# Attention maxima of two heads in the row halves of TensorE, transposed reciprocals, and one more leading column tile in a diffusion block

## The chip, the core and the metric

The kernel runs on one core of a Trainium2 chip. The metric is device time in microseconds for one execution. TensorE (PE in the profile) multiplies; loading its stationary operand is a separate instruction (PEld). VectorE (DVE), ScalarE (ACT) and GpSimd (POOL) do the elementwise work, and SyncE (SP) issues nearly all DMAs. Each engine runs its own instructions in program order and waits on semaphores for the others. TensorE writes into PSUM, eight banks of 128 partitions by 512 float32 words.

## What is computed

One layer of a block with two groups of heads, 1024 latent tokens, 256 context tokens, width 1024, head size 64. Group A is softmax attention with 8 query heads and 2 key heads; group B is a retention with 8 heads in chunks of 128. Both outputs go through one output projection, and a SwiGLU feed-forward network (FFN) of hidden width 2816 follows. All is float32. Cut to what matters here:

```
def gqa_block(q, k, v):
    qg = q.reshape(B, Q, ATTN_KV_HEADS, GQA_GROUP, HEAD_DIM)
    s = jnp.einsum('bqkgd,btkd->bkgqt', qg, k) * ATTN_SCALE
    p = jax.nn.softmax(s, axis=-1)
    o = jnp.einsum('bkgqt,btkd->bqkgd', p, v)
...
def swiglu(h, w_ffn_in, w_ffn_out):
    a, b = jnp.split(h @ w_ffn_in, 2, axis=-1)
    return (jax.nn.silu(a) * b) @ w_ffn_out
```

## The kernel before

Operands of the large products are split into a high part (rounded to float32r, which TensorE multiplies in one pass) and the remainder, the low part. Three products high·high, high·low and low·high add up to one float32 product (`mm3`, line 131). Plain float32 operands are also used in places, and then one matmul of the program is two records in the trace.

The stages that matter here, with their place in the profiled execution:

- **The last projections** (297.5 to 358.5 us). The input projection runs in column groups; the last of them are woven, step by step, with `front(0)` and `front(1)`. `front(h)` prepares one attention head. It splits the queries (`q3`, layout low, high, one more column), transposes them to `t1` (64 rows of low parts above 64 rows of high parts, line 581), and then finds for each of 1024 queries a maximum over all 1280 keys: 24 matmuls of `t1` against `K1`, whose 128 rows hold the high part of the keys twice (line 589), each followed by a reduction on VectorE (line 590). The negated maxima go into the last column of `q3` (lines 592 and 593), and a second set of transposes makes `t2` (line 598), whose 65th row carries the maximum into the scores.
- **Attention and retention** (358.5 to 704 us). Four pairs of heads `r`, two halves of queries, ten key tiles: `score` makes two accumulating matmuls per head (lines 625 and 626), ScalarE takes the exponential, `weigh` multiplies with the values, both heads of a pair in the two column halves of TensorE (line 634), `sums` adds up the denominators, and `normalise` turns the reciprocals over with a matmul against the identity (line 662) and multiplies. `front` for the next pair and the retention of four pairs of heads (`retain`, lines 741 to 812) are woven between. The retention multiplies two heads in the two row halves of TensorE (line 796, 64 rows each) and uses column halves too (lines 741, 808, 810).
- **Output projection** (704 to 804.5 us), for eight token tiles `mix_in`, `mix_out`, `residual`, `modulate`.
- **FFN** (from 804.5 us). The first matrix is multiplied with a scheme of seven products on half-size blocks per column tile `j`. Two of the seven (`first_product`, `second_product`) need only the tokens as they are; the other five need sums of token blocks (`Tx`), which VectorE splits first. Column tiles 0, 1 and 2 have their first two products done ahead of the rest, "leading"; the weights of tile 2 are in tiles named `lead`.

The instruction order is not written out. Code is written in the order of generators that `weave` advances by shares (`N_FR` is the number of steps of a `front`), and a scheduler then orders each engine's instructions by its own timeline; `tc.issue_after(x)` only makes the following instructions come later than x. All short-lived PSUM tiles (`sbank`) share four banks.

Of the kernel before, what the change touches and what calls it, by code (L numbers as in the profile page):

```python
# [11 lines left out]
F32 = mybir.dt.float32  # L12
F32R = mybir.dt.float32r
AF = mybir.ActivationFunctionType
ALU = mybir.AluOpType
# [4 lines left out]
P = 128  # L20
# [87 lines left out]
def hybrid_block(ctx: ExitStack, tc, x, c, cx, c_ctx, w_mod, b_mod, g_pre_mix, g_post_mix,  # L108
# [5 lines left out]
    def f(ap):  # L114
        return ap.bitcast(F32)
# [440 lines left out]
    def falloc(first, shape, dt, tag, bufs):  # L556
        if first == 1:
            return kvp.tile(shape, dt, name=f"{tag}b")
        if first == 0:
            return gp.tile(shape, dt, tag="g", name=tag)  # L560
        return atf.tile(shape, dt, tag=tag, name=tag, bufs=bufs)

    def front(h):

        kv = h // 4
        if h % 2 == 0:
            qs2[h // 2] = falloc(h, [P, LT, P], F32, "qs", 1)
            nc.sync.dma_start(out=qs2[h // 2], in_=d_p[0:N_LAT, h * HD:(h + 2) * HD].rearrange("(t p) n -> p t n", p=P))
        q3 = falloc(h, [P, LT, 2 * HD + 2], F32R, "q3", 2)
        qs = qs2[h // 2][:, :, (h % 2) * HD:(h % 2 + 1) * HD]  # L570
        S.copy(out=q3[:, :, HD:2 * HD], in_=qs)
        hold["q"] = V.tensor_tensor(out=q3[:, :, 0:HD], in0=qs, in1=f(q3[:, :, HD:2 * HD]), op=ALU.subtract)
# [4 lines left out]
        fr[h] = (t1, t2)  # L577
        for b in range(2):
            tb = sbank(F32R)
            for i in range(4):  # L580
                T.transpose(out=tb[:, i * P:(i + 1) * P], in_=q3[:, b * 4 + i, 0:P], identity=identr)
            S.copy(out=t1[:, b * 512:(b + 1) * 512], in_=f(tb))
            yield
        mx = small.tile([P, LT, 4], F32, tag="mx", name="mx")
        nm = small.tile([P, LT], F32, tag="nm", name="nm")
# [6 lines left out]
        V.tensor_reduce(out=nm, in_=mx[:, :, 0:3], axis=AX.X, op=ALU.max, negate=True)  # L592
        V.tensor_copy(out=q3[:, :, 2 * HD:2 * HD + 1], in_=nm.unsqueeze(2))
        yield
        for b in range(2):
            tb = sbank(F32R)
            for i in range(4):
                T.transpose(out=tb[:HD + 1, i * P:(i + 1) * P], in_=q3[:, b * 4 + i, HD:2 * HD + 1], identity=identr)
            S.copy(out=t2[:, b * 512:(b + 1) * 512], in_=f(tb[:HD + 1]))
            yield  # L600
# [253 lines left out]
    N_FR, N_RT, N_AT = 13, 47, 40  # L854
    attend = attention()
    retained = chain(*(retain(r) for r in range(4)))
    for n, fronts in ((N_AT, [2, 3]), (N_AT, [4, 5]), (N_AT, [6, 7])):
        n_r = n * 4 * N_RT // (3 * N_AT) + 1
        weave((islice(attend, n), n), (chain(*(front(h) for h in fronts)), len(fronts) * N_FR + 1),
              (islice(retained, n_r), n_r))  # L860
# [48 lines left out]
    up = ffs.enter_context(tc.tile_pool(name="up", bufs=3))  # L909
# [6 lines left out]
    def mix_in(t):  # L916

        tsl = slice(t * P, (t + 1) * P)
        rn = wk3.tile([P, 512], F32, tag="rn", name="rn", bufs=1)
        nc.sync.dma_start(out=rn, in_=d_r[tsl, :])  # L920
        mt = wk3.tile([P, 4, P], F32, tag="mt", name="mt", bufs=1)
        nc.sync.dma_start(out=mt, in_=d_m.rearrange("(k p) n -> p k n", p=P)[:, :, tsl])
        tb = sbank()
        for i in range(4):
            T.transpose(out=tb[:, i * P:(i + 1) * P], in_=rn[:, i * P:(i + 1) * P], identity=ident)
        rT = rTs[t] = wk3.tile([P, 2, KT, P], F32R, tag="rT", name="rT")
        split(rT[:, 0, 0:4], rT[:, 1, 0:4], mt, V)
        split(rT[:, 0, 4:8], rT[:, 1, 4:8], tb.rearrange("p (k n) -> p k n", n=P), S)
# [146 lines left out]
    raws[2] = [quarter(i, 2) for i in range(2)]  # L1075
# [7 lines left out]
    As[2] = [(hl[:, i, 0], hl[:, i, 1]) for i in range(2)]  # L1083
    N_EARLY = 3
# [15 lines left out]
    first_product(2)  # L1100
    second_product(2)
# [184 lines left out]
```

## Time and profile before

| what | value |
|---|---|
| time, median of 3 runs | 1494.71 us (1490.71 to 1501.16) |
| time of the profiled execution | 1494.64 us |
| its span, first to last instruction | 1492.9 us |
| TensorE busy | 1425.1 us (95%) |
| VectorE busy | 849.8 us (57%) |
| ScalarE busy | 525.8 us (35%) |
| GpSimd busy | 496.5 us (33%) |
| chain that ended last, TensorE's share | 80% |

Between span and time lie 1.7 us. A record's length is the latency of one instruction; matmuls overlap, so the pace of TensorE is read from the distance between starts.

### The profile page before, as it was taken

To read this page: it belongs to the slowest core of one execution; us is meant where nothing else is said; L and a number is where in the kernel's file an instruction comes from. 1 tells how busy PE (TensorE), PEld (TensorE's weight loads), DVE (VectorE), ACT (ScalarE), POOL (GpSimd) and SP (SyncE) were. 2 spreads that over 40 slices of the span, in tenths; PEclk is the share of its full clock that TensorE was granted. 3 is DMA by queue.
4 is the path that set the end of the run, shared out by engine and by line. 5 is a ranking of instruction groups with operands and counts; after the bars stand their busy time and mean duration, and the time that the engine had idled before them with its cause. 6 is when DMAs were issued, how large, how long until landed. Compare 5 with 4: busy or idle time off the path is not lost.

```text
span 1492.9 us, 19980 instructions
## 1 busy us (share of the span) xinstructions
PE 1425.1 (95%) x7354; PEld 1074.7 (72%) x7354; DVE 849.8 (57%) x1447; ACT 525.8 (35%) x1143; POOL 496.5 (33%) x402
## 2 busy tenths in 40 slices
PE   6999999898999999998998899999999999999997
PEld 2787877787555555544887688888888888888886
DVE  2666767545766677665556655444444454445445
ACT  3750221223655545455346423222222231113112
POOL 0112246401553636352016454444444430002003
PEclk9999999999999989999999999999999999999999
DMA  9456634314102111014334132222222225444562
GB/s 352 148 173 208 198 119 136 124 50 127 46 26 82 40 47 40 23 49 141 114 113 141 57 99 85 85 85 83 75 83 85 76 88 187 152 148 143 189 204 113
DMA packets 140624, 169.12 MB, mean 113 GB/s; under 512 B 8992, under 2 KB 90608, under 8 KB 140528
## 3 DMA queue, kind: packets, MB, share of 16 engines
q1 hardware_dynamic: 139680, 167.61, 34.6%
q8 instruction: 58, 0.95, 0.3%
q10 hardware_dynamic: 848, 0.25, 0.1%
q14 instruction: 38, 0.31, 0.1%
HBM read 132.17 MB, written 35.65 MB: 112 GB/s over the span
## 4 chain that ended last, share of the span: by engine, by line
PE 80%; DVE 8%; DMA 6%; ACT 2%; issue 2%; POOL 1%; SPq 0%; DVEq 0%; POOLq 0%; ACTq 0%
PE pb L131 48%; PE sb L131 15%; PE o L634 4%; PE sb L625 3%; PE sb L589 2%; DMA wm<-in_w_mod 2%; PE sb L626 2%; DMA raw<-in_w_out 1%; DVE ss L779 1%; PE r L796 1%; DVE mx L590 1%; PE r L741 1%; PE sb L808 1%; DMA rv<-d_p 1%; DMA raw<-in_w_in 1%
## 5 line engine op out<-in xcount | busy, mean ns | idle before, releaser
L131 PE MATMUL pb<-T,w 128*128 128x512 f32 x1320 | 315.2, 393 | 4.8 <-DVE T L126 2.1
L131 PEld LDWEIGHTS pb<-T,w 128*128 128x128 f32 x1320 | 246.9, 187 | 63.0 <-ACT w L125 2.6
L131 PE MATMUL pb<-whi,hT 128*128 128x512 f32 (+1 forms) x896 | 263.0, 374 | 5.3 <-ACT whi L125 3.6
L131 PEld LDWEIGHTS pb<-whi,hT 128*128 128x128 f32 x896 | 162.3, 190 | 40.3 <-ACT whi L125 4.5
L131 PE MATMUL pb<-wlo,hT 128*128 128x512 f32 (+1 forms) x448 | 165.4, 372 | 2.6 <-DVE wlo L126 2.6
L590 DVE TENSOR_REDUCE mx<-sb 128x1 f32<-128x512 f32 (+1 forms) x192 | 107.0, 594 | 53.4 <-PE sb L589 52.6
L126 DVE TENSOR_TENSOR w<-w1raw,w 128x512 fp32r<-128x512 f32 x152 | 123.3, 867 | 15.7 <-ACT w L125 15.7
L131 PE MATMUL sb<-B,w 128*128 128x512 f32 x504 | 124.9, 391 | 0.8 <-ACT u L1063 0.8
L125 ACT CAST w<-w1raw 128x512 fp32r<-128x512 f32 x152 | 83.7, 618 | 96.0 <-POOL w1raw L1010 94.4
L627 ACT ACTIVATE p<-sb 128x512 f32<-128x512 f32 x160 | 92.9, 599 | 68.2 <-PE sb L626 67.2
L131 PEld LDWEIGHTS sb<-B,w 128*128 128x128 f32 x504 | 94.4, 188 | 22.2 <-ACT u L1063 1.2
L682 POOL TENSOR_TENSOR acc<-acc,p 128x1024 f32<-128x1024 f32 x30 | 71.5, 2383 | 107.4 <-ACT p L627 103.1
L1142 POOL TENSOR_TENSOR g<-g,c 128x512 f32<-128x512 f32 x22 | 34.7, 1579 | 212.0 <-DVE c L1141 187.0
L131 PE MATMUL pb<-w,ah 128*128 128x512 f32 x328 | 101.7, 389 | 0.0
L131 PE MATMUL sb<-w,ah 128*128 128x512 f32 x328 | 101.5, 389 | 0.0
L131 PEld LDWEIGHTS pb<-wlo,hT 128*128 128x128 f32 x448 | 85.4, 191 | 19.4 <-DVE wlo L126 3.5
L634 PE MATMUL o<-p,VV 128*64 128x512 f32 x320 | 89.3, 637 | 5.1 <-ACT p L627 5.0
L176 POOL TENSOR_TENSOR ss<-ss,mhalf 128x1 f32<-128x1 f32 x26 | 15.0, 582 | 235.4 <-DVE ss L175 235.4
L125 ACT CAST w<-raw 128x512 fp32r<-128x512 f32 x41 | 25.4, 623 | 168.6 <-PE pb L131 152.8
L131 PE MATMUL pb<-woh,rT 128*128 128x512 f32 x256 | 82.3, 401 | 0.0
L125 DVE CAST ah<-ra 128x1024 fp32r<-128x1024 f32 x41 | 28.5, 698 | 88.7 <-PE pb L131 88.5
L319 POOL TENSOR_TENSOR st<-r,r 128x256 f32<-128x256 f32 (+1 forms) x32 | 42.3, 1323 | 90.0 <-DVE r L318 64.2
(258 smaller groups left out, 2470.3 us busy)
## 6 DMA issues: line engine op xcount, KB each, us to landing
w1raw<-in_w_ffn_in SPq DMA_DIRECT2D x92, 256.0 KB, 3.4
ra<-d_a SPq DMA_DIRECT2D x41, 512.0 KB, 4.3
wm<-in_w_mod SPq DMA_DIRECT2D x64, 256.0 KB, 3.2
raw<-in_w_ffn_out SPq DMA_DIRECT2D x41, 256.0 KB, 3.7
d_p<-st SPq DMA_DIRECT2D x34, 256.0 KB, 2.0
wm<-in_w_mod SPq DMA_DIRECT2D x16, 512.0 KB, 7.1
raw<-in_w_in SPq DMA_DIRECT2D x32, 256.0 KB, 4.3
d_a<-g SPq DMA_DIRECT2D x22, 256.0 KB, 2.0
```

What stands on the lines that cost most here:

```text
L125: a = S.copy(out=hi, in_=src) if hi_eng is S else hi_eng.tensor_copy(out=hi, in_=src)
L126: return a, V.tensor_tensor(out=lo, in0=src, in1=f(hi), op=ALU.subtract)
L131: T.matmul(acc, lhsT=a, rhs=b, start=first and a is ah and b is bh, stop=last and a is al, skip_group_check=onto)
L319: G.tensor_tensor(out=dst, in0=t1, in1=t2, op=ALU.add)
L589: T.matmul(sb[:, :n], lhsT=t1[:, t * P:(t + 1) * P], rhs=K1[:, kv, k0:k0 + n], start=True, stop=True)
L590: V.tensor_reduce(out=mx[:, t, j:j + 1], in_=sb[:, :n], axis=AX.X, op=ALU.max)
L625: T.matmul(sb, lhsT=K1[:, h // 4, ksl], rhs=t1[:, qsl], start=True, stop=False)
L626: T.matmul(sb, lhsT=K2[:, h // 4, ksl], rhs=t2[:, qsl], start=False, stop=True)
L627: S.activation(out=p[:, :, h % 2, :], in_=sb.rearrange("p (i n) -> p i n", n=P), func=AF.Exp)
L634: return T.matmul(st["o"][j * HD:(j + 1) * HD, :], lhsT=VV[kt][:, r // 2, :], rhs=p[:, :, j, :], start=(kt == 0), stop=(kt == AT - 1))
L682: eng.tensor_tensor(out=st["a"], in0=prev if kt == 1 else st["a"], in1=p, op=ALU.add)
L1142: G.tensor_tensor(out=g0, in0=g0, in1=c21, op=ALU.mult)
```

## The change

Four edits.

First, `front` now prepares the two heads of a pair together. The queries of the odd head are laid out high, low, high, so that its `t1` has the high parts in rows 0 to 63, while the even head keeps them in rows 64 to 127. The maximum is taken from high part times high part alone, 64 rows deep: one matmul in the lower row half for the even head (line 595), one in the upper row half for the odd head (line 598), into two PSUM banks. There are as many matmuls and reductions as before. Four empty steps stand between the maxima and the second transposes. The query tiles `qs` and `q3` of the even heads come from the pool `gp`. Second, `normalise` uses the transpose form of the matmul. Third, `mix_in` takes its two input tiles from the pool `xq` with 34 buffers, not from two single buffers. Fourth, a column tile 3 leads the FFN too.

```diff
-    def front(h):
-        kv = h // 4
...
-        t1 = falloc(h, [P, N_LAT], F32R, "t1", 4)
-        t2 = falloc(h, [HD + 1, N_LAT], F32R, "t2", 4)
...
-        for t in range(LT):
-            for j, (k0, n) in enumerate(((0, 512), (512, 512), (1024, 256))):
-                sb = sbank()
-                T.matmul(sb[:, :n], lhsT=t1[:, t * P:(t + 1) * P], rhs=K1[:, kv, k0:k0 + n], start=True, stop=True)
-                V.tensor_reduce(out=mx[:, t, j:j + 1], in_=sb[:, :n], axis=AX.X, op=ALU.max)
-            yield
+    def front(r):
+        kv, es = r // 2, (2 * r, 2 * r + 1)
...
+        S.copy(out=q3[0][:, :, HD:2 * HD], in_=qs[0])
+        hold["q"] = V.tensor_tensor(out=q3[0][:, :, 0:HD], in0=qs[0], in1=f(q3[0][:, :, HD:2 * HD]), op=ALU.subtract)
         yield
+        for i in (0, 2):
+            S.copy(out=q3[1][:, :, i * HD:(i + 1) * HD], in_=qs[1])
+        V.tensor_tensor(out=q3[1][:, :, HD:2 * HD], in0=qs[1], in1=f(q3[1][:, :, 0:HD]), op=ALU.subtract)
         yield
...
+        rows = (slice(HD, P), slice(0, HD))
+        for t in range(LT):
+            for c_, (k0, n) in enumerate(((0, 512), (512, 512), (1024, 256))):
+                sbs = [sbank() for _ in range(2)]
+                first = T.matmul(sbs[0][:, :n], lhsT=fr[es[0]][0][rows[0], t * P:(t + 1) * P], rhs=K1[rows[0], kv, k0:k0 + n],
+                                 start=True, stop=True)
+                with tc.issue_after(first.ins):
+                    T.matmul(sbs[1][:, :n], lhsT=fr[es[1]][0][rows[1], t * P:(t + 1) * P], rhs=K1[rows[1], kv, k0:k0 + n],
+                             start=True, stop=True)
+                for j in range(2):
+                    V.tensor_reduce(out=mx[j][:, t, c_:c_ + 1], in_=sbs[j][:, :n], axis=AX.X, op=ALU.max)
+                yield
...
+        for _ in range(4):
             yield
...
-    N_FR = 15
-    weave((project, 18), (chain(front(0), front(1)), 2 * N_FR))
+    N_FR = 38
+    weave((project, 18), (front(0), N_FR))
...
         for i in range(4):
-            T.matmul(rb[:, i * P:(i + 1) * P], lhsT=st["r"][:, 2 * i:2 * i + 2, :].rearrange("p a d -> p (a d)"), rhs=ident,
-                     start=True, stop=True)
+            T.transpose(out=rb[:, i * P:(i + 1) * P], in_=st["r"][:, 2 * i:2 * i + 2, :].rearrange("p a d -> p (a d)"),
+                        identity=ident)
...
-        rn = wk3.tile([P, 512], F32, tag="rn", name="rn", bufs=1)
+        rn = quad(F32, "rn").rearrange("p k n -> p (k n)")
...
-        mt = wk3.tile([P, 4, P], F32, tag="mt", name="mt", bufs=1)
+        mt = quad(F32, "mt")
...
-    raws[2] = [quarter(i, 2) for i in range(2)]
+    for j in (2, 3):
+        raws[j] = [quarter(i, j) for i in range(2)]
...
+    As[3] = [split2(x) for x in raws[3]]
+    first_product(2)
+    second_product(2)
...
-    first_product(2)
-    second_product(2)
+    first_product(3)
+    second_product(3)
```

How TensorE's order moves is shown at three places. The first is in the last projections. `pb<-whi,hT` and `pb<-wlo,hT` are projections with all 128 rows. Before, one maximum of one head (line 589, all 128 rows) stands between them:

```order
L589 MATMUL sb<-K_83,t_2771 128x512
L131 MATMUL pb<-whi,hT 128x256 x2
L131 MATMUL pb<-wlo,hT 128x256
L131 MATMUL pb<-whi,hT 128x256
L589 MATMUL sb<-K_83,t_2771 128x512
```

Of the changed kernel, where line 595 is the lower row half and line 598 the upper:

```order
L595 MATMUL sb<-K_83,t_2747 128x512
L131 MATMUL pb<-whi,hT 128x256
L131 MATMUL pb<-wlo,hT 128x256
L131 MATMUL pb<-whi,hT 128x256
L598 MATMUL sb<-K_83,t1b 128x512
L131 MATMUL pb<-whi,hT 128x256
```

The two halves of a pair do not stand side by side here: projections stand between them, and so it is for all 24 pairs of this stretch.

The second place is in attention and retention. Before, with line 589 for the maxima, lines 625 and 626 for the scores (all rows and columns), lines 634 and 741 in column halves:

```order
L589 MATMUL sb<-K_83,t_3577 128x512 x2
L589 MATMUL sb<-K_83,t_3577 128x256
L741 MATMUL r<-rv,qk_3554 64x64 x4
L741 MATMUL r<-rv,qk_3568 64x64 x4
L625 MATMUL sb<-t_2771,K_83 128x512
L626 MATMUL sb<-t_2772,K_84 128x512
L634 MATMUL o<-p,VV_88 64x512 x2
```

Of the changed kernel, where the scores are lines 642 and 643, and the column halves lines 651 and 758:

```order
L595 MATMUL sb<-K_83,t_4548 128x256
L758 MATMUL r<-rv,qk_5139 64x64 x4
L598 MATMUL sb<-K_83,t_4550 128x256
L758 MATMUL r<-rv,qk_5154 64x64 x4
L642 MATMUL sb<-t_3573,K_83 128x512
L643 MATMUL sb<-t_3574,K_84 128x512
L595 MATMUL sb<-K_83,t_4548 128x512
L598 MATMUL sb<-K_83,t_4550 128x512
L651 MATMUL o<-p,VV_85 64x512 x2
```

Of the 72 pairs of this stretch 43 stand side by side (32 of them 512 columns wide, 11 of them 256), as the second pair here; 29 are parted by other work, as the first.

The third place is where the FFN begins, before and then of the changed kernel. `lead` is column tile 2, `xn` the last token tile before its transposes, `w_7832` to `w_7837` column tile 3, and `T` the split sums:

```order
L970 MATMUL sb<-ident,xn 128x128 x8
L131 MATMUL sb<-B_6869,lead 128x512 x12
L131 MATMUL sb<-B_6870,lead 128x512 x12
L131 MATMUL pb_7960<-T_7824,w_7907 128x512
```

```order
L131 MATMUL sb<-B_6873,lead 128x512 x12
L987 MATMUL sb<-ident,xn 128x128 x8
L131 MATMUL sb<-B_6873,w_7832 128x512 x2
L131 MATMUL sb<-B_6873,w_7833 128x512
...
L131 MATMUL sb<-B_6874,lead 128x512 x12
L131 MATMUL sb<-B_6874,w_7836 128x512 x2
L131 MATMUL sb<-B_6874,w_7837 128x512
...
L131 MATMUL pb_8005<-T_7869,w_7952 128x512
```

The first product of tile 2 has moved ahead of the transposes of `xn`, and 24 matmuls of tile 3 stand ahead of the first product with `T`.

## Rows read from the trace of the kernel before

**Rows 1.** The page: span, and busy time of the engines.

```profile
span 1492.9 us, 19980 instructions
PE 1425.1 (95%) x7354; PEld 1074.7 (72%) x7354; DVE 849.8 (57%) x1447; ACT 525.8 (35%) x1143; POOL 496.5 (33%) x402
```

**Rows 2.** Windows by stage: us, busy time of each engine, granted clock, DMA.

```profile
297.50:358.50 61.00, 61.00 (x379) 54.07 (x377) 29.20 (x56) 12.11 (x31) 0.00 (x0) 1.00 0.14 48
358.50:704.00 345.50, 320.26 (x2299) 181.29 (x2300) 234.06 (x421) 188.43 (x408) 166.24 (x128) 0.96 0.21 60
704.00:804.50 100.50, 100.50 (x472) 82.16 (x470) 53.31 (x94) 42.79 (x107) 19.38 (x22) 0.98 0.39 129
804.50:849.90 45.40, 35.63 (x147) 27.05 (x145) 35.24 (x42) 28.45 (x59) 26.30 (x18) 0.96 0.20 58
```

**Rows 3.** Timeline of PE in attention: start, length, line, operation, tiles, shape, count.

```profile
401.46 0.50 PE L625 MATMUL sb<-t,K 128*128 128x512 f32 x1
401.80 0.39 PE L626 MATMUL sb<-t,K 65*128 65x512 f32 x1
402.03 0.62 PE L589 MATMUL sb<-K,t 128*128 128x512 f32 x2
402.58 0.49 PE L796 MATMUL r<-qT,kT 64*128 64x128 f32 x4
403.00 0.34 PE L808 MATMUL sb<-rv,im 128*64 128x64 f32 x4
```

**Rows 4.** Timeline of PE, one maximum between two matmuls in row halves.

```profile
475.73 0.49 PE L796 MATMUL r<-qT,kT 64*128 64x128 f32 x2
476.14 0.39 PE L589 MATMUL sb<-K,t 128*128 128x256 f32 x1
476.46 0.48 PE L796 MATMUL r<-qT,kT 64*128 64x128 f32 x2
```

**Rows 5.** Timeline of PE in the last projections.

```profile
349.68 0.39 PE L589 MATMUL sb<-K,t1b 128*128 128x512 f32 x1
349.91 0.28 PE L131 MATMUL pb<-wlo,hT 128*128 128x256 f32 x1
```

**Rows 6.** Timeline of PE: reciprocals by matmul, and transposes of `xn`.

```profile
656.78 1.16 PE L662 MATMUL sb<-ident,rw 128*128 128x128 f32 x8
657.70 0.51 PE L625 MATMUL sb<-t,K 128*128 128x512 f32 x1
...
803.67 1.04 PE L970 MATMUL sb<-ident,xn 128*128 128x128 f32 x8
804.46 5.71 PE L131 MATMUL sb<-B,w 128*128 128x512 f32 x24
```

**Rows 7.** Waits of PE, 297.5 to 704 us: total us, times, longest.

```profile
PE sb L598 <- DVE q L593: 6.4, 4, 2.8
...
PE sb L581 <- issue: 1.5, 1, 1.5
...
PE sb L598 <- DVE q3b L593: 1.4, 1, 1.4
PE sb L625 <- DVE mx L590: 1.4, 2, 1.2
```

**Rows 8.** Timeline of PE where the FFN begins; waits in brackets.

```profile
811.00 5.75 PE L131 MATMUL sb<-B,w 128*128 128x512 f32 x24 [0.82 <-ACT u L1063]
820.23 1.97 PE L970 MATMUL sb<-ident,xn 128*128 128x128 f32 x8 [3.48 <-DVE xn L960]
821.85 3.76 PE L131 MATMUL sb<-B,lead 128*128 128x512 f32 x12
...
831.86 5.85 PE L131 MATMUL pb<-T,w 128*128 128x512 f32 x24 [2.06 <-DVE T L126]
```

**Rows 9.** Timeline of DVE at the same place.

```profile
814.46 1.78 DVE L126 TENSOR_TENSOR lead<-w1raw,lead 128x512 fp32r<-128x512 f32 x1
...
818.43 1.75 DVE L960 TENSOR_SCALAR xn<-xt,s 128x1024 f32<-128x1024 f32 x1
```

More of the change, by code (lines that the diff above doesn't have):

```diff
@@ L558, in falloc @@
             return kvp.tile(shape, dt, name=f"{tag}b")
-        if first == 0:
+        if first == 0 or tag in ("qs", "q3"):
             return gp.tile(shape, dt, tag="g", name=tag)
         return atf.tile(shape, dt, tag=tag, name=tag, bufs=bufs)
-    def front(h):
-        kv = h // 4
[L566 to L572, printed above, removed]
+    def front(r):
+        kv, es = r // 2, (2 * r, 2 * r + 1)
+        pick = (0, 1) if r == 0 else (None, None)
+        qs2[r] = falloc(pick[0], [P, LT, P], F32, "qs", 1)
+        nc.sync.dma_start(out=qs2[r], in_=d_p[0:N_LAT, r * P:(r + 1) * P].rearrange("(t p) n -> p t n", p=P))
+        qs = [qs2[r][:, :, j * HD:(j + 1) * HD] for j in range(2)]
+        q3 = [falloc(pick[0], [P, LT, 2 * HD + 1], F32R, "q3", 1), falloc(pick[1], [P, LT, 3 * HD + 1], F32R, "q3o", 1)]
+        S.copy(out=q3[0][:, :, HD:2 * HD], in_=qs[0])
+        hold["q"] = V.tensor_tensor(out=q3[0][:, :, 0:HD], in0=qs[0], in1=f(q3[0][:, :, HD:2 * HD]), op=ALU.subtract)
@@ L593, in front @@
[L593 to L600, printed above, removed]
-    N_FR = 15
+        for j in range(2):
+            fr[es[j]] = (falloc(pick[j], [P, N_LAT], F32R, "t1", 4), falloc(pick[j], [HD + 1, N_LAT], F32R, "t2", 4))
@@ new lines, in front @@
+        for j in range(2):
+            for b in range(2):
+                tb = sbank(F32R)
+                for i in range(4):
+                    T.transpose(out=tb[:, i * P:(i + 1) * P], in_=q3[j][:, b * 4 + i, 0:P], identity=identr)
+                S.copy(out=fr[es[j]][0][:, b * 512:(b + 1) * 512], in_=f(tb))
+                yield
+        mx = [small.tile([P, LT, 4], F32, tag="mx", name="mx") for _ in range(2)]
+        rows = (slice(HD, P), slice(0, HD))
[7 more added lines that the diff above has]
+                             start=True, stop=True)
+                for j in range(2):
+                    V.tensor_reduce(out=mx[j][:, t, c_:c_ + 1], in_=sbs[j][:, :n], axis=AX.X, op=ALU.max)
+                yield
@@ new lines, in front @@
+        for j in range(2):
+            nm = small.tile([P, LT], F32, tag="nm", name="nm")
+            e0 = (2 + j) * HD
+            V.tensor_reduce(out=nm, in_=mx[j][:, :, 0:3], axis=AX.X, op=ALU.max, negate=True)
+            V.tensor_copy(out=q3[j][:, :, e0:e0 + 1], in_=nm.unsqueeze(2))
+        for _ in range(4):
+            yield
+        for j in range(2):
+            for b in range(2):
+                tb = sbank(F32R)
+                e0 = (1 + j) * HD
+                for i in range(4):
+                    T.transpose(out=tb[:HD + 1, i * P:(i + 1) * P], in_=q3[j][:, b * 4 + i, e0:e0 + HD + 1], identity=identr)
+                S.copy(out=fr[es[j]][1][:, b * 512:(b + 1) * 512], in_=f(tb[:HD + 1]))
+                yield
@@ L852, in retain @@
         yield
-    N_FR, N_RT, N_AT = 13, 47, 40
+    N_RT, N_AT = 47, 40
     attend = attention()
     retained = chain(*(retain(r) for r in range(4)))
-    for n, fronts in ((N_AT, [2, 3]), (N_AT, [4, 5]), (N_AT, [6, 7])):
+    for n, r in ((N_AT, 1), (N_AT, 2), (N_AT, 3)):
         n_r = n * 4 * N_RT // (3 * N_AT) + 1
-        weave((islice(attend, n), n), (chain(*(front(h) for h in fronts)), len(fronts) * N_FR + 1),
+        weave((islice(attend, n), n), (front(r), N_FR),
               (islice(retained, n_r), n_r))
```

11 lines of the change are left out of this document (1 added, 10 removed).

## The prediction

> **What bounds the kernel now.** I read the busy times first, then a table of windows by stage, then the timeline of TensorE. TensorE is busy for 95% of the span, VectorE for 57% [rows 1]. By stage [rows 2] TensorE is busy all 61.0 us of the last projections and all 100.5 us of the output projection; in attention and retention it idles 25.2 of 345.5 us, and where the FFN begins 9.8 of 45.4 us. VectorE, ScalarE and GpSimd are far below that, so what TensorE is made to do longer, the kernel does longer, and only the 25.2 and the 9.8 us can be won back by better order.
>
> But a busy TensorE is not one that streams columns, and the distance between starts shows what it loses. In one mode a 512-column float32r matmul starts 0.23 us after the one before (401.80 to 402.03), a 256-column one takes 0.12 [rows 3, 5]. Now look at what happens between full matmuls and those in halves. The second maximum of the pair at 402.03 starts at 402.26; the row halves at 402.58 start 0.32 after it, 0.09 late. The score at 401.46, first after column halves, lasts 0.50 instead of 0.39, and its successor starts 0.34 later, not 0.23: it waited 0.11 for weights that could not be loaded ahead. So **each change between full array, row halves and column halves costs about 0.09 + 0.11 = 0.20 us** [rows 3]. A single 256-column maximum between two row-half matmuls holds TensorE for 0.32 us instead of 0.12, the same 0.20 [rows 4].
>
> The same rows show that row halves do run together: one head alone takes 0.49 us (two records), both heads also take 0.49 (four records) [rows 3, 4]. Those are plain float32; no row shows a float32r matmul of 64 rows.
>
> **The change, step by step.**
>
> *Maxima in the last projections.* There are 48 of them, 32 of 512 and 16 of 256 columns, and all 24 pairs are parted by projections, so nothing overlaps: a half-array matmul of 512 columns streams as long as a whole one. Each half stands alone between full matmuls; in the order I count 94 changes of mode where there were none. 94 × 0.20 = **+18.8 us**. No other engine hides it, since TensorE had no idle time there. Its bounds: 0, if float32r halves switched free of charge, and +18.8.
>
> *The seam to attention.* Before, TensorE waited 1.4 us for the negated maxima of head 1, then 1.5 us for the transposes of the next head [rows 7]. Now the maxima end some 35 projection matmuls before the stage does, and the load of the next queries stands ahead of the last spill on SP's queue instead of behind it. I take **−2.5 us** (0 to −2.9). What is late next is the first exponential, as before.
>
> *Maxima in attention.* The order has 414 changes of mode in this stretch where there were 324: 80 more into row halves, 12 more into column halves, two fewer into the full array. 90 × 0.20 = **+18.0 us**. The 43 pairs that stand together save one matmul each: 32 × 0.23 + 11 × 0.12 = **−8.7 us** (0, if float32r halves do not overlap). With 29 parted pairs and an array that was busy 93%, the loss is about twice the gain.
>
> Here the trace is to be held against a page of the Trainium skill. TensorEngine Tiling (Array Packing), section Theoretical Speedup, gives up to a factor 2 for a contraction of 64 rows. By that factor alone all 96 pairs would save 64 × 0.23 + 32 × 0.12 = 18.6 us and the sum below would end at 1460. Its section Key Properties says that changing the tiling mode, not just the tile, drains TensorE, without a price; rows 3 agree and give it.
>
> *The four empty steps.* In attention TensorE waited 6.4 us, four times, for the negated maxima before the second transposes [rows 7]. Now a dozen matmuls of other work stand between. I take all **−6.4 us** (0 to −6.4); what it runs into next is the release of a PSUM bank.
>
> *A new wait.* Each pair takes two of the four shared banks, and the reduction of the odd head waits for a half that may stand a retention step later. Behind it on VectorE's queue the other reductions, the retention's multiplications and the additions of denominators; scores wait for the banks. Before, TensorE's waits of scores for reductions came to 1.4 us [rows 7]. Bounds: −1.4, if the looser spacing frees them, to +6.4, if it becomes as bad as the wait just removed. I take 0: before, three maxima in a row could take three banks.
>
> *Transposes instead of matmuls.* Four calls of the reciprocals take 0.92 us (656.78 to 657.70, eight records); eight transposes take 0.79 us (803.67 to 804.46), so four take 0.40 [rows 6]. Eight times 0.5 = **−4.0 us** (0, if VectorE, not TensorE, is waited for).
>
> *Odd heads' extra cast* (ScalarE, four times) and *mix_in's buffers*: nothing. ScalarE has 157 us idle in attention; uncovered, four casts at its mean of 188.43/408 = 0.46 us would cost 1.8 us. The output projection has no idle time of TensorE that an earlier load could fill [rows 2].
>
> *The leading tile.* Before, TensorE ended the second products at 816.75, waited 3.48 us for `xn`, and then 2.06 us for `T` before 831.86 [rows 8]. Now the first product of tile 2 (12 × 0.23 = 2.8 us) fills the first gap, since its weights were split by 816.24 [rows 9]. VectorE pays for it: a split of `lead` stands ahead of `xn`, and the two of tile 3 ahead of the last `T`, 1.78 us each at the pace of rows 9. So `xn` comes 1.8 us later, and `T` 2 to 3.5. TensorE has 24 × 0.23 = 5.5 us more to do before `T`, work that is then missing from the loop. 5.5 less 2.5 is **−3.0 us**; bounds 0 and −5.5.
>
> The sum, against the profiled execution's own 1494.6 us (its span of 1492.9 plus 1.7; the median is 1494.7, the same within 0.1): 1494.6 + 18.8 − 2.5 + 18.0 − 8.7 − 6.4 − 4.0 − 3.0 = **1506.8, so 1507 us**, 0.8% slower. A difference below 1%, some 15 us, can hardly be told from none in this kernel.
>
> **The rivals.** *Free switching.* The price was read where plain float32 in row halves stood beside float32r; if float32r on both sides switched without drain and with weights ahead, both positive terms fall away: 1506.8 − 36.8 = 1470 us, faster. It decides from about 0.04 us a switch on: below it the time is under 1480. Against it speaks that the gap appears on every side of rows 3 and 4, whichever form comes next. *Half price*, 0.10 us, where only drain or only weights count: 1506.8 − 18.4 = 1488. *Halves that do not overlap*: no row shows 64 rows of float32r; then 8.7 us come back, 1516, and with the bank wait's 6.4 as well 1522. For overlap speak the four records of rows 3. *Clock.* In attention the mean granted clock is 0.96 [rows 2]; as the two levels are 2.4 and 1.2 GHz, some 8%, 27.6 us, ran at the lower. If all of it went, 13.8 us would come back: 1493. If as much again ran at the lower level: 1521. The low stretches come after waits, some of which go and some of which move, so I take no change.
>
> By the page's factor of 2 without a switching price the time would be 1460; that is the free-switching rival with every pair together, and it has no chance of its own, since 53 pairs are apart in the order.
>
> **How the numbers follow.** Forecast, 1498 to 1517: 0.62. Free switching: 0.06. Half price: 0.10. No overlap or bank waits, 1516 to 1524: 0.16. The clock beyond that, either way: 0.06. The range 1487 to 1521 leaves out free switching, the top of the fourth case and part of the last, 0.15 to 0.2 in all. Faster by over 1% (below 1480): free switching and a bit, 0.07. Slower by over 1% (above 1509.6): no overlap, 0.16, a third of the forecast's own 0.62, and 0.03 of the clock: 0.40. Within 1%: 0.53.
>
> **What would show it.** The last projections should take 77 to 80 us where they took 61, with TensorE still busy throughout, and a lone half-array maximum should hold TensorE for about 0.6 us among projections (0.23 now). Pairs that stand together should start within hundredths of a us. In attention TensorE's idle time should fall from 25 us to about 17 while the stretch stays within some 5 us of its length. The wait of 3.48 us before `xn` should be gone, that for `T` remain. The prediction is wrong if a lone half shows no gap on either side, or if scores wait for reductions by several us.

## The result and the profile after

| what | before | after |
|---|---|---|
| median of 20 runs each | 1494.49 us (1488.74 to 1501.39) | 1503.89 us (1496.6 to 1538.91) |
| ratio after to before, 95% interval | | 1.0054 (1.0039 to 1.0069) |
| profiled execution: time, span | 1494.64 us, 1492.9 us | 1507.39 us, 1505.5 us |
| mean granted clock of the profiled execution | 0.980 | 0.971 |
| median granted clock of the runs | 0.978 (60 executions of other lots) | 0.976 |

The change makes the kernel some 0.5% to 0.6% slower. That is clear of the noise (the interval leaves out 1), and less than the 1% that the prediction drew as its line. The ratios, and all of the table with the twelve experiments below, leave out executions more than 1.5% slower than the fastest of their kernel. The engines of the changed kernel, from its page:

```profile
span 1505.5 us, 19898 instructions
...
PE 1451.1 (96%) x7322; PEld 1067.1 (71%) x7322; DVE 843.3 (56%) x1447; ACT 527.3 (35%) x1147; POOL 499.2 (33%) x402
```

TensorE (PE) is busy 26 us longer than in [rows 1], the other engines as before. The windows of the changed kernel by stage (last projections, attention and retention, output projection, start of the FFN); the columns are those of [rows 2]:

```profile
295.20:373.70 78.50, 78.50 (x382) 54.91 (x381) 32.15 (x59) 11.94 (x30) 0.00 (x0) 1.00 0.13 42
373.70:720.00 346.30, 330.61 (x2268) 173.55 (x2266) 222.59 (x417) 190.02 (x411) 167.13 (x128) 0.92 0.20 59
720.00:819.50 99.50, 99.50 (x464) 81.01 (x463) 53.93 (x94) 41.95 (x104) 22.06 (x22) 0.99 0.37 126
819.50:862.10 42.60, 38.73 (x170) 31.26 (x169) 35.56 (x41) 28.10 (x58) 22.22 (x15) 0.96 0.26 75
```

Set beside [rows 2], the last projections take about 18 us more with TensorE busy throughout. Attention takes as long as before within 2.4 us (346.05 us from the first score to the first output projection, 343.65 before), although TensorE idles 15.7 us in it and no longer 25.2. What it no longer idles, it is busy longer, and its granted clock there is 0.92, not 0.96. The FFN is about 3 us shorter. Taken from the starts of the stages: last projections +18.0, seam −2.0, attention +2.4, FFN −2.9 (up to its second matrix), everything before the last projections −2.5, the rest −0.3; together the 12.7 us between the two profiled executions. The −2.5 stands in work that the change doesn't touch. In kernels whose work up to there is the same, that place is reached between 295.2 and 299.2 us, so it is scatter of one execution.

The price of a change of mode can now be read where a float32r half stands alone. TensorE in the last projections of the changed kernel (start, length; line 595 is the lower row half):

```profile
320.75 0.63 PE L131 MATMUL pb<-whi,hT 128*128 128x512 f32 x2
321.31 0.50 PE L595 MATMUL sb<-K,t 64*128 64x512 f32 x1
321.74 0.50 PE L131 MATMUL pb<-wlo,hT 128*128 128x512 f32 x1
322.08 0.63 PE L131 MATMUL pb<-whi,hT 128*128 128x512 f32 x2
322.64 0.49 PE L598 MATMUL sb<-K,t1b 64*128 64x512 f32 x1
```

Two whole matmuls of 0.23 us start at 320.75; the half starts 0.56 after them, 0.10 late. Its successor starts 0.43 after it, 0.20 late, and the one behind that 0.34 later, 0.11 late for its weights. A lone half thus costs 0.41 us beside its own 0.23. And where two halves stand together, in attention:

```profile
395.05 0.50 PE L642 MATMUL sb<-t1b,K 128*128 128x512 f32 x1
395.39 0.39 PE L643 MATMUL sb<-t2b,K 65*128 65x512 f32 x1
395.71 0.50 PE L595 MATMUL sb<-K,t 64*128 64x512 f32 x1
395.71 0.49 PE L598 MATMUL sb<-K,t 64*128 64x512 f32 x1
396.14 0.69 PE L758 MATMUL r<-rv,qk 128*64 128x64 f32 x16
```

Both halves start at 395.71 and the next instruction 0.43 later, as after a single half. So two float32r row halves run together, and here the second is free.

The waits of TensorE from the last projections to the end of attention (total us, times, longest) have no row for the second transposes, now line 615, which stood at the top of [rows 7] with 6.4 us:

```profile
PE sb L679 <- ACT rw L673: 3.3, 2, 2.8
PE r L758 <- DMA rv<-d_p: 2.8, 2, 1.6
PE o L651 <- ACT p L644: 2.1, 5, 0.6
PE sb L642 <- ACT p L644: 1.8, 2, 1.6
...
PE sb L598 <- DVE mx L601: 0.7, 2, 0.3
```

Waits for the reductions of the maxima come to less than 1 us: the new wait for banks did not appear. Where the FFN begins, TensorE waits 3.04 us for `T` and, as before, 0.8 us for `u`; the wait for `xn` of [rows 8] is gone:

```profile
832.24 2.91 PE L131 MATMUL sb<-B,lead 128*128 128x512 f32 x12
834.99 1.03 PE L987 MATMUL sb<-ident,xn 128*128 128x128 f32 x8
...
844.06 0.63 PE L131 MATMUL pb<-T,w 128*128 128x512 f32 x2
847.73 2.59 PE L131 MATMUL pb<-T,w 128*128 128x512 f32 x8 [3.04 <-DVE T L126]
```

**The clock makes the executions of one kernel differ.** Each execution has its mean granted clock, and within each kernel of the table below the time falls as the clock rises, by 0.9 to 1.5 us for 0.001 (lines fitted to each kernel's runs). To compare work and not luck, the table also gives each kernel's mean time carried to a clock of 0.976 at 1.2 us for 0.001, with twice the standard error. The spread of the slopes adds up to 0.3 us for each 0.001 between a kernel's clock and 0.976, some 3 us for e3_lone and e4_lead3. The kernel before ran beside the experiments in three lots, and is the same in all within this precision.

| kernel | median, us | ratio to before, 95% | median clock | at clock 0.976, us |
|---|---|---|---|---|
| before (60 runs, three lots) | 1493.7 | | 0.978 | 1496.9 ± 0.7 |
| after | 1502.7 | 1.0054 (1.0039 to 1.0069) | 0.976 | 1502.8 ± 1.1 |
| e1_full | 1492.4 | 0.9978 (0.9956 to 0.9999) | 0.974 | 1489.4 ± 1.0 |
| e2_full_front | 1487.5 | 0.9976 (0.9941 to 1.0010) | 0.975 | 1485.7 ± 1.2 |
| e3_lone | 1523.6 | 1.0212 (1.0168 to 1.0255) | 0.968 | 1514.0 ± 1.6 |
| e4_lead3 | 1521.0 | 1.0173 (1.0134 to 1.0213) | 0.967 | 1508.7 ± 3.0 |
| e8_rv2 | 1482.6 | 0.9941 (0.9914 to 0.9967) | 0.978 | 1484.8 ± 1.3 |
| e10_matmul | 1507.1 | 1.0082 (1.0059 to 1.0105) | 0.980 | 1511.0 ± 0.5 |
| e11_full_rv2 | 1482.5 | 0.9913 (0.9886 to 0.9940) | 0.980 | 1485.6 ± 1.9 |
| e12_before_rv2 | 1501.1 | 1.0055 (1.0035 to 1.0075) | 0.976 | 1501.5 ± 0.9 |
| e13_nosteps | 1521.4 | 1.0161 (1.0127 to 1.0195) | 0.969 | 1512.1 ± 1.6 |
| e14_before_T | 1501.6 | 1.0033 (1.0004 to 1.0062) | 0.972 | 1495.5 ± 1.2 |

The two atomic kernels (e6_atomic, e7_two_pairs) are left out of the table: their clock lies too far from 0.976. So of the 9 us between the medians of the kernel before and the changed one, 5.9 ± 1.3 us remain at equal clock; some 2 to 3 us go with a clock that is lower by 0.002.

### The profile page after: what moved, and what is told of

The parts are those of the page before. It is cut to its first block, busy times and chain, and to the rows that moved or that the text cites. A ratio compares the mean times of both kernels' runs of the same rounds, so it can differ in the third digit from the quotient of the medians.

```text
span 1505.5 us, 19898 instructions
## 1 busy us (share of the span) xinstructions
PE 1451.1 (96%) x7322; PEld 1067.1 (71%) x7322; DVE 843.3 (56%) x1447; ACT 527.3 (35%) x1147; POOL 499.2 (33%) x402
## 4 chain that ended last, share of the span: by engine, by line
PE 86%; DVE 5%; DMA 5%; ACT 2%; issue 1%; POOL 1%; DVEq 0%; ACTq 0%; POOLq 0%
PE pb L131 51%; PE sb L131 15%; PE o L651 4%; PE sb L642 3%; PE sb L595 2%; PE sb L643 2%; DVE ss L796 1%; DMA wm<-in_w_mod 1%; PE sb L598 1%; DMA raw<-in_w_out 1%; PE r L813 1%; PE r L758 1%; PE sb L825 1%; DMA raw<-in_w_in 1%; DMA rv<-d_p 1%
## 5 line engine op out<-in xcount | busy, mean ns | idle before, releaser
L601 DVE TENSOR_REDUCE mx<-sb 128x1 f32<-128x512 f32 (+1 forms) x192 | 110.3, 597 | 87.1 <-PE sb L595 48.3
L651 PE MATMUL o<-p,VV 128*64 128x512 f32 x320 | 93.1, 662 | 2.1 <-ACT p L644 2.1
L176 POOL TENSOR_TENSOR ss<-ss,mhalf 128x1 f32<-128x1 f32 x26 | 15.4, 594 | 233.5 <-DVE ss L175 233.5
```

The source lines that it names most:

```text
L601: V.tensor_reduce(out=mx[j][:, t, c_:c_ + 1], in_=sbs[j][:, :n], axis=AX.X, op=ALU.max)
L651: return T.matmul(st["o"][j * HD:(j + 1) * HD, :], lhsT=VV[kt][:, r // 2, :], rhs=p[:, :, j, :], start=(kt == 0), stop=(kt == AT - 1))
```

## The experiments

The theory: a change of mode costs about 0.20 us wherever it stands, and halves that stand together overlap. The rivals: switching is free, halves do not overlap, and the lower clock of attention is what costs. The runs start from the changed kernel, except where the kernel before is named.

**Whole rows everywhere**, with the same instruction order on every engine:

```diff
-        rows = (slice(HD, P), slice(0, HD))
+        rows = (slice(0, P), slice(0, P))
```

> The changed kernel with all its edits and its instruction order on every engine, but each maximum again runs over all 128 rows (the low parts multiply too). In the order the changes of TensorE's mode fall from 94 to 0 in the last projections and from 414 to 350 in attention. By the theory (0.20 us a change, halves that stand together overlap): 94 x 0.20 = 18.8 us and 64 x 0.20 = 12.8 us come back, and the 8.7 us that 43 adjacent pairs saved are lost: 1503.9 - 18.8 - 12.8 + 8.7 = 1481 us; the last projections 60 us (78.5 with halves). If switching were free: 1503.9 + 8.7 = 1513. If halves did not overlap: 1503.9 - 31.6 = 1472. If it is the row halves that bring the lower clock of attention (granted 0.92, before 0.96): 0.04 x 346 = 14 us more come back, 1467, with a clock of 0.96 there; if they do not, the clock there stays near 0.92.

**Whole rows in the last projections only**, row halves in attention, the order again the same:

```diff
-        rows = (slice(HD, P), slice(0, HD))
+        rows = (slice(0, P), slice(0, P)) if r == 0 else (slice(HD, P), slice(0, HD))
```

> The changed kernel with 128 rows only for the first pair of heads, whose maxima lie in the last projections; attention keeps its row halves. Order unchanged. Theory: the 94 changes of mode of the last projections go, 94 x 0.20 = 18.8 us: 1485 us, the last projections 60 us, attention unchanged at 346 us. Half the price a change: 1494. Free switching: 1504. The difference between this run and the one with 128 rows everywhere is what row halves bring or cost in attention: +4.1 us for them by the theory's price (64 x 0.20 - 8.7), -8.7 with free switching, +18 if the clock goes with them.

Windows of the last projections and of attention, first with whole rows everywhere, then with whole rows in the last projections only:

```profile
296.00:356.30 60.30, 60.30 (x381) 53.81 (x380) 31.10 (x59) 11.96 (x30) 0.00 (x0) 1.00 0.16 53
356.60:701.00 344.40, 323.67 (x2263) 178.05 (x2262) 227.50 (x417) 189.46 (x411) 167.78 (x128) 0.94 0.20 59
```

```profile
296.50:356.80 60.30, 60.30 (x381) 53.77 (x379) 31.10 (x59) 11.95 (x30) 0.00 (x0) 1.00 0.16 53
357.10:716.40 359.30, 342.77 (x2265) 178.04 (x2263) 224.12 (x417) 190.32 (x411) 166.57 (x128) 0.88 0.19 57
```

The last projections take 60.3 us in both, against 78.4 in the changed kernel (295.2 to 373.6): 18.1 us for 94 changes, **0.19 us each**, and free switching is out. At equal clock the second kernel is 17.1 ± 1.6 us faster than the changed one, the same 18 us within its error. The two kernels of this section differ in attention alone, by 64 changes of mode and 43 pairs. By the theory's price, row halves cost 12.8 − 8.7 = 4.1 us there; at equal clock they **gain 3.7 ± 1.6 us**. That misses the expectation by 8 us. The windows show a part of the reason: with whole rows TensorE idles 20.7 us in attention (344.4 less 323.67), in the changed kernel 15.7. So some five us of the switching seem to lie where TensorE waited anyway. Uncarried, the two are equal on average (ratios 0.9978 and 0.9976), because the executions with row halves had the lower clock (0.972 on average, 0.974 with whole rows).

**The kernel before with lone halves.** No pairing and no reordering of the heads, only 64 rows instead of 128:

```diff
-                T.matmul(sb[:, :n], lhsT=t1[:, t * P:(t + 1) * P], rhs=K1[:, kv, k0:k0 + n], start=True, stop=True)
+                T.matmul(sb[:, :n], lhsT=t1[HD:P, t * P:(t + 1) * P], rhs=K1[HD:P, kv, k0:k0 + n], start=True, stop=True)
```

> The kernel before with one edit: each maximum multiplies only the 64 rows of high parts, one head after the other, always in the lower row half, so that nothing can overlap; three maxima in a row share their changes of mode. In the order there are 80 changes in the last projections (0 before) and 383 in attention (324). Theory at the price the last projections showed (18.1 us / 94 = 0.19 us a change): 80 x 0.19 = 15.4 us in the last projections, 59 x 0.19 = 11.4 us in attention, 1494.5 + 26.8 = 1521 us. Rival: in attention TensorE waits for others anyway and the changes fill those waits; then the last projections still take 76 us and the rest moves by less than 5: 1510 to 1514. Rival: the price came with the reordering of the pair and not with the switch: 1495. Further rival: the lower granted clock comes with the row halves, also here, 0.92 or below in attention (0.96 before): 14 us on top of either.

The last projections of the kernel before, and then these two windows with lone halves:

```profile
297.80:358.10 60.30, 60.30 (x377) 53.81 (x376) 28.82 (x55) 11.84 (x30) 0.00 (x0) 1.00 0.14 49
...
297.15:372.96 75.81, 75.81 (x377) 54.67 (x375) 30.22 (x55) 11.83 (x30) 0.00 (x0) 1.00 0.11 39
375.50:731.80 356.30, 338.14 (x2295) 184.03 (x2292) 228.80 (x417) 189.23 (x407) 164.52 (x128) 0.91 0.20 58
```

The last projections take 75.8 us, 15.4 more than before (60.4 with both ends in) for 80 changes: 0.19 us each once more, so the price belongs to the switch and not to the new order. At equal clock the whole kernel is 17.1 ± 1.7 us slower. That leaves 1.7 us (and no closer than some 3 us, as the kernel's clock lies 0.009 from 0.976) for the 59 further changes in attention, where the price would be 11.4, although nothing overlaps in this kernel and nothing pays for them. TensorE's idle time in attention falls from 25.2 to 18.2 us (356.3 less 338.14): the waits take 7 us of the changes. This fits the rival that TensorE waits for others anyway. The clock of 0.91 in attention and a median of 1523.6 came on top, as its further rival had it.

**Halves forced side by side**, one pair, then two pairs at a time, in an atomic section (the second kernel allocates four banks for two column pieces and puts the four matmuls into one section):

```diff
-                first = T.matmul(sbs[0][:, :n], lhsT=fr[es[0]][0][rows[0], t * P:(t + 1) * P], rhs=K1[rows[0], kv, k0:k0 + n],
-                                 start=True, stop=True)
-                with tc.issue_after(first.ins):
-                    T.matmul(sbs[1][:, :n], lhsT=fr[es[1]][0][rows[1], t * P:(t + 1) * P], rhs=K1[rows[1], kv, k0:k0 + n],
-                             start=True, stop=True)
+                with tc.tile_critical():
+                    for j in range(2):
+                        T.matmul(sbs[j][:, :n], lhsT=fr[es[j]][0][rows[j], t * P:(t + 1) * P], rhs=K1[rows[j], kv, k0:k0 + n],
+                                 start=True, stop=True)
```

> The changed kernel with the two halves of each pair forced to stand side by side (one atomic section for both matmuls). All 96 pairs are adjacent; changes of mode 46 in the last projections (94 in the changed kernel), 383 in attention (414). Theory: 48 x 0.20 = 9.6 us and 31 x 0.20 = 6.2 us fewer changes, and 53 more pairs overlap: 32 x 0.23 + 21 x 0.12 = 9.9 us. 1503.9 - 25.7 = 1478 us, more by waits for the second bank if those appear (up to 6.4). Free switching: 1503.9 - 9.9 = 1494. Halves that do not overlap: 1503.9 - 15.8 = 1488. In the last projections a pair should cost about 0.23 + 0.40 = 0.63 us where two whole matmuls cost 0.46.

> The changed kernel with two pairs (four matmuls, four banks) in one atomic section. Changes of mode 16 in the last projections (94), 316 in attention (414). Theory: 176 x 0.20 = 35.2 us fewer changes and 9.9 us more overlap: 1503.9 - 45.1 = 1459 us, if nothing waits for banks. Rival: each section needs all four shared banks, so TensorE waits while up to four reductions of 0.6 us run: at 36 sections in attention, 1 us each would take 36 us back and end at about 1495. Free switching: 1494 at best. Halves that do not overlap: 1469 and the bank waits.

They took 1665.15 us (ratio 1.1149, 1.1124 to 1.1174) and 1603.69 us (1.0747, 1.0714 to 1.0780), far outside every expectation, at median clocks of 0.918 and 0.935. The groups of VectorE in the first of them show where:

```profile
L600 DVE TENSOR_REDUCE mx<-sb 128x1 f32<-128x512 f32 (+1 forms) x192 | 106.8, 598 | 222.2 <-PEq L595 222.2
```

The reductions wait 222 us for TensorE's sequencer at the section's end (PEq), not for a matmul. TensorE in turn waits in front of the sections: 21.5 us without a releaser in the profile, 12.2 us behind GpSimd's work for the retention, only 8.8 us behind reductions. So the section itself seems to hold up both engines, and for the whole kernel both runs are inconclusive. TensorE's timeline among the projections still shows what halves in a group are worth. Two pairs of 512 columns in one section of the second kernel, whose halves all stand in line 598:

```profile
306.45 0.63 PE L131 MATMUL pb<-whi,hT 128*128 128x512 f32 x2
307.53 0.50 PE L598 MATMUL sb<-K,t 64*128 64x512 f32 x1 [0.45 <-issue]
307.53 0.50 PE L598 MATMUL sb<-K,t1b 64*128 64x512 f32 x1
307.87 0.39 PE L598 MATMUL sb<-K,t 64*128 64x512 f32 x1
307.87 0.39 PE L598 MATMUL sb<-K,t1b 64*128 64x512 f32 x1
308.35 0.50 PE L131 MATMUL pb<-wlo,hT 128*128 128x512 f32 x1
308.68 0.63 PE L131 MATMUL pb<-whi,hT 128*128 128x512 f32 x2
```

The pairs overlap, which saves 2 × 0.23 us. But the second pair starts 0.11 late, the next whole matmul 0.25 late and the one behind it 0.10 late. From 307.53 to 308.68, less the projection's own 0.23, the four halves hold TensorE for 0.92 us, as long as four whole matmuls, and the wait of 0.45 us in front comes on top. A single pair of the first kernel holds it for 0.69 us (306.20 to 307.12, less 0.23), where 0.63 was expected and two whole ones take 0.46. So among whole matmuls a pair loses and two pairs break even at best. That longer groups would gain is not shown. The stretch as a whole can't be set beside the 60.3 us of whole rows, as only 32 of its 48 maxima lie in it; the others come in attention.

**The waits in front of the low clock.** In the changed kernel's attention the lower of the two clock levels (1.2 GHz, 0.50) holds in four stretches before its end. The two longest are these windows; below them TensorE's timeline where the first begins, behind a wait for the retention's values:

```profile
514.70:535.20 20.50, 20.50 (x87) 9.27 (x85) 7.58 (x14) 6.95 (x20) 12.64 (x12) 0.50 0.00 1
...
555.60:569.30 13.70, 13.70 (x36) 6.08 (x32) 5.00 (x14) 5.91 (x11) 4.54 (x2) 0.50 0.00 0
```

```profile
511.56 0.38 PE L595 MATMUL sb<-K,t 64*128 64x256 f32 x1
513.12 0.69 PE L758 MATMUL r<-rv,qk 128*64 128x64 f32 x16 [1.18 <-DMA rv<-d_p]
513.73 0.38 PE L598 MATMUL sb<-K,t 64*128 64x256 f32 x1
514.04 1.39 PE L651 MATMUL o<-p,VV 128*64 128x512 f32 x4
515.36 0.80 PE L642 MATMUL sb<-t,K 128*128 128x512 f32 x1
515.95 0.63 PE L643 MATMUL sb<-t,K 65*128 65x512 f32 x1
```

After a wait of 1.18 us the score's successor starts 0.59 us after it instead of 0.34. A second buffer takes that wait away, first in the kernel with halves in attention only:

```diff
-        vn = rt.tile([P, AT, P], F32, tag="rv", name="rv")
+        vn = rt.tile([P, AT, P], F32, tag="rv", name="rv", bufs=2)
```

> The kernel with 128 rows in the first pair and row halves in attention, plus a second buffer for the retention's values, so that their load no longer waits for the previous pair's last matmul. It takes away two waits of TensorE (1.5 and 1.1 us), behind which the granted clock fell to 0.5 for 31 us each in the profile of that kernel. If these waits start the low stretches: no low stretch begins there, the executions near 1500 vanish, median 1482 to 1485 us (1494 without the edit) at a mean clock of 0.976 or above. If the low clock comes from the row halves themselves, whatever waits stand before: two groups of times remain, near 1484 and 1500 to 1506, and a median of 1490 or above; the buffer itself is then worth at most 2.6 us.

The median fell from 1487.5 to 1482.6 us at a clock of 0.978 (0.975), while at equal clock the two are the same (−0.9 ± 1.8). That looks like the theory of the waits, but its announced sign, that the executions near 1500 vanish, failed. Executions of 1498.8, 1502.0 and 1511.7 us still occur, and in the profiled one a low stretch begins with no wait of over 0.5 us in the 4 us before it. TensorE had been busy for 11.67 of 12.5 us, with retention in row halves among its work. Of the two waits on which the expectation was built, only the one of 1.1 us stands in front of its low stretch (it ends at 502.8, the stretch begins at 503.9). The one of 1.5 us ends at 424.0, and the stretch put down to it begins at 452.7, behind a wait of 0.93 us for ScalarE. The two windows with the second buffer:

```profile
455.00:467.50 12.50, 11.67 (x63) 5.87 (x61) 11.43 (x22) 11.37 (x25) 8.70 (x9) 1.00 0.45 128
467.50:494.80 27.30, 27.30 (x131) 14.24 (x128) 7.57 (x13) 8.33 (x17) 6.21 (x3) 0.50 0.03 10
```

The same buffer with whole rows everywhere, and alone in the kernel before:

> The changed kernel with 128 rows in every maximum and the second buffer for the retention's values; against the run with row halves in attention and the same buffer it differs in that alone (335 changes of mode in attention against 412, same order). If row halves bring the low clock: a mean clock near 0.978, no executions more than 8 us above the lowest, and a median below 1483. If the waits bring it and the buffer has taken them away for both: the clock is the same as with halves, and the time is 4 us higher, as the two kernels without the buffer stood at equal clock (1489.3 to 1485.2 at 0.976): 1486 to 1488.

> The kernel before with only the second buffer for the retention's values. The waits for that load (0.76 and 0.88 us there) go. If the buffer acts by its waits alone: 1.6 us at most, 1492 to 1494. If it also keeps the clock up: the clock was 0.978 already, so no more than that. A gain of 5 us or more would say that the gain of the buffer in the other kernels was not the clock.

With whole rows the median is 1482.5 us at a clock of 0.980. At equal clock it is 0.8 ± 2.3 us above the one with halves, not the 4 us expected, and one execution of six still took 1497.7 us. So the clock is not settled by either: neither these waits nor the row halves alone decide it. These two kernels are the fastest of the study, 0.6% and 0.9% below the kernel before. In the kernel before the buffer made things 4.6 us *worse* at equal clock. The waits for the load went, but the scheduler reordered attention. Another wait came up, 5.0 us in three pieces, the longest 3.4, so that TensorE idles 26.1 us there where it idled 25.2; and it is busy 3.2 us longer, with nine more changes of mode, which by their price are 1.8 us of it (an estimate). The rest is open:

```profile
PE sb L625 <- DVE oh L664: 5.0, 3, 3.4
PE sb L598 <- DVE q L593: 3.8, 3, 2.8
```

**The smaller edits**, each undone in the changed kernel. Three leading tiles:

```diff
-    for j in (2, 3):
-        raws[j] = [quarter(i, j) for i in range(2)]
+    raws[2] = [quarter(i, 2) for i in range(2)]
...
-    As[3] = [split2(x) for x in raws[3]]
-    first_product(2)
-    second_product(2)
...
-    first_product(3)
-    second_product(3)
+    first_product(2)
+    second_product(2)
```

> The changed kernel with three leading column tiles as before, all else unchanged up to the FFN. Theory: +3.0 us (bounds 0 and +5.5): 1506.9 us at the same mean clock; the wait for xn of some 3.5 us is back, and the time from the last matmul of the output projection to the first product with split sums stays near 25 us with 24 matmuls fewer in it. Rival, the tile only moves work that is done anyway: 1504, unchanged.

At equal clock it is 5.9 ± 3.2 us slower, where 3.0 was expected with a bound of 5.5; the wait for `xn` is back. The trace gives a closer reading: from the last matmul of the output projection to the first product with `ah` (of the FFN's second matrix) it is 456.5 us, in the changed kernel 453.8 and before 456.7. So the tile is worth 2.6 to 2.9 us. TensorE's longest wait at the FFN's start in the kernel with three tiles:

```profile
PE sb L987 <- DVE xn L977: 3.2, 1, 3.2
```

Its attention is that of the changed kernel, instruction for instruction, and yet its median clock was 0.967 where the changed kernel's was 0.976, and its median 1521 us. A clock seen in one lot is therefore no property of a kernel.

No empty steps:

```diff
-        for _ in range(4):
-            yield
...
-    N_FR = 38
+    N_FR = 34
```

> The changed kernel without the four empty steps between the maxima and the second transposes; 518 changes of mode (521). Theory: TensorE again waits for the negated maxima before the second transposes, four waits of 6.4 us in the kernel before, three of them in attention here and one in the last projections hidden: +4 to +6 us at equal clock, 1508 to 1510. Rival: with both heads of a pair prepared together the reductions of the two end at once and the wait is longer, up to 10 us. Rival: the scheduler fills the gap itself: 1504.

It is 9.3 ± 1.9 us slower at equal clock, but by another way than announced. There is no wait of the second transposes in it; the idle time of TensorE in attention is 20.8 us (15.7) and lies at the exponentials and the retention's copies. These are its longest waits there:

```profile
PE sb L640 <- ACT p L642: 3.4, 4, 1.6
PE sb L677 <- ACT rw L671: 3.2, 2, 2.8
PE o L649 <- ACT p L642: 2.7, 4, 1.2
```

Matmuls in `normalise` again, and transposes alone in the kernel before:

```diff
-            T.transpose(out=rb[:, i * P:(i + 1) * P], in_=st["r"][:, 2 * i:2 * i + 2, :].rearrange("p a d -> p (a d)"),
-                        identity=ident)
+            T.matmul(rb[:, i * P:(i + 1) * P], lhsT=st["r"][:, 2 * i:2 * i + 2, :].rearrange("p a d -> p (a d)"), rhs=ident,
+                     start=True, stop=True)
```

> The changed kernel with plain matmuls against the identity in normalise again (eight records of 0.11 us where the transposes have four of about half). Theory: 8 x 0.5 = 4.0 us back, 1507.9 us at the same mean clock. Rival: the result waits for the reciprocals or VectorE anyway, 1504 to 1505, unchanged.

> The kernel before with transposes in place of matmuls in normalise, nothing else. Theory: eight times 0.5 us, 1494.5 - 4.0 = 1490.5 at equal clock; undoing the edit in the changed kernel cost 8 us at equal clock. If 8 us is the edit's worth: 1486.5. If it was the order of the work around it that moved there: 1490 to 1491. If the result waits for the reciprocals anyway: 1494.

Undone, it costs 8.2 ± 1.2 us; done alone, it gains 1.4 ± 1.4. The 4.0 us forecast lie between the two, and neither agrees with them. In both the order of attention moved with the edit (three and eight changes of mode more), so neither run prices the transposes alone. In the changed kernel's trace four of them hold TensorE for 0.51 us (698.62 to the next start at 699.13), against 0.92 in [rows 6], which makes 8 × 0.41 = 3.3 us.

## Why the prediction was right, and where its steps were not

1507 us was forecast and 1503.9 measured. The sign, the size and the reading "within 1%" hold. But two steps of the sum were wrong in opposite directions: attention came out some 6 to 7 us cheaper than forecast, and the clock, put at nothing, took most of that back (about 10 us in the profiled execution, 2 to 3 between the medians). At equal clock the change costs 5.9 ± 1.3 us where the steps add up to 12.2. That the sum came so close is in this part luck.

| step | forecast, us | shown, us |
|---|---|---|
| maxima in the last projections | +18.8 | +18.0 by the stage, −18.1 undone |
| seam to attention | −2.5 | −2.0 |
| attention, 90 changes of mode less 43 pairs | +18.0 − 8.7 | −3.7 ± 1.6 for 64 of the changes and all pairs, −0.8 ± 2.3 for 77 with the second buffer, at equal clock |
| four empty steps, with the new bank wait | −6.4 + 0 | idle time 25.2 to 15.7, of which 5.0 is switching that fills waits |
| transposes | −4.0 | about −3.3 by the rows; between −1.4 and −8.2 by the runs |
| leading tile | −3.0 | −2.9 by the stage; undone, +2.6 by the stage and +5.9 ± 3.2 by the runs |
| clock in attention | 0 | about +10 in the profiled execution, +2 to +3 between the medians |

*Right.* The price of 0.20 us a change, read from plain float32 halves, holds for float32r, and in a stage where TensorE never waits it adds up one to one. Halves that stand side by side start within hundredths of a us. The bank wait stayed away, the seam closed, and the wait for `xn` went while that for `T` remained. A lone half was forecast to hold TensorE for about 0.6 us; it holds it for 0.23 + 0.41 = 0.64.

*The step "Maxima in attention" was too dear by some 8 us.* It multiplied 90 changes by the price of a stage without idle time. Attention has idle time, and changes that fall into waits cost less. Between kernels of one order, TensorE idles 5.0 us less with halves (20.7 us with whole rows, 15.7 with halves), and 5.6 us less in the pair with the second buffer (18.5 and 12.9). With lone halves it was 7.0 us. The lower clock doesn't explain it: in three profiles with the changed kernel's attention TensorE idles 15.7, 15.3 and 16.5 us at clocks of 0.92, 0.91 and 0.88. That the changes filled these waits is read from single executions. The rest of the gap, about 3 us, stays open. The prediction knew both numbers, 93% busy and 25.2 us idle, and used them for the waits that it wanted to remove, not for the changes that it added.

*The step "Clock" was wrong by about 10 us in the profiled execution.* It put the clock at no change. In [rows 2] the mean clock in attention is 0.96, here 0.92. Stretch by stretch, 55 us of attention ran at the lower level (10.2, 6.8, 20.5, 13.7 and 3.9), where 31 us did before (10.2, 10.2, 3.4, 3.4 and 3.5): 24 us more. By the fitted 1.2 us for 0.001 of a 1500 us span, which is 3 us at the lower level, a us there costs 0.4 us, so 24 us cost about 10. Without them attention would have taken some 336 us where it took 343.65: −7.6, while the steps summed to −1.1. Between the medians of many runs the clock differs less (0.976 to 0.978). Which work or which wait makes it fall is not settled.

*"Four empty steps"* was right in direction, and the wait it names did go; what the steps are worth came out larger when undone (9.3 us), with other waits than the one named and another order.

The rivals: free switching and halves that don't overlap are refuted by the windows and the timeline. Half price would have been near for attention as a result but not as a mechanism, since the rows show the full price there too. The Trainium skill, TensorEngine Tiling (Array Packing), section Key Properties, says that changing the tiling mode drains TensorE. The trace agrees: 0.10 us going into a half and 0.20 coming out of it, and 0.11 for the weights behind.

## What to carry to other kernels

A half-height matmul between whole ones costs about 0.4 us more than a whole one. Two pairs of halves side by side, four matmuls, only break even there. In attention, beside work that is in halves already and with an engine that waits at times, they gained 1 to 4 us. Price an added stall with the idle time of the stage it lands in: in full where TensorE never waits, and less the waits it can fill elsewhere. Where a scheduler sets the order, an edit of 2 to 4 us reorders everything around it by as much. Compare kernels of identical order (here by changing only the rows that are multiplied), and carry times to one clock before taking differences below 1%.

## What the runs showed of the chip that was not expected

- The granted clock differs between executions of one program by up to 0.02 to 0.03, and each 0.001 goes with about 1.2 us. The same attention, instruction for instruction, had a median clock of 0.976 in one lot and 0.967 in another.
- Most low stretches of attention begin within a few us of a wait of TensorE of 0.8 to 3 us, but not every such wait is followed by one, and one stretch of 27.3 us began with no wait over 0.5 us in the 4 us before it.
- A section that is atomic for the scheduler cost far more than it ordered: VectorE waited 222 us for TensorE's sequencer with 96 sections.
